# mLSTM encoder layer: new places for the mLSTM branch's blocks and the merged branches, and a longer, yielding filler

## The chip, the cores and the metric

The kernel runs on one core of one Trainium2 chip. The core's engines work side by side, each through its own queue in order: TensorE (PE, matmuls; PEld is its weight load), VectorE (DVE), ScalarE (ACT), GpSimd (POOL) and SyncE (SP), which here only issues DMAs. The metric is the device time of one execution in microseconds (us); lower is better.

## The reference, cut to what matters

One encoder layer over 1024 + 256 tokens (a prompt and a sample) of width 1024. An input projection feeds two branches; branch A is a gated convolution, branch B a chunkwise mLSTM that runs forward and backward, with 4 heads of 256 and chunks of 128 tokens (8 + 2 chunks). Each branch is projected, gated and added, and one output projection with a residual follows.

```python
h = rms_norm(x, norm_g) * (1.0 + scale) + shift
p = h @ w_in
cb, cc, cx, cz, q, k, v, o, mz, gpre, gmerge = split_combined(p)
y_conv = cb * centred_dwconv3(cc * cx, conv_w, conv_b) * silu(cz)
hm = h_fwd + h_bwd    # two mlstm_chunkwise scans over chunks of 128
hm = hm * rsqrt(mean(hm * hm) + EPS) * mh_norm_g
y_m = sigmoid(o) * hm * silu(mz)
merged = g_conv * (y_conv @ w_proj_conv) + g_mlstm * (y_m @ w_proj_mlstm)
return x + gate * (merged @ w_out)      # then a last rms_norm
```

In a scan each chunk reads the state C left by the chunk before it (`q @ C`) and then updates it, `C = decay * C + k^T (w v)`; inside a chunk, scores `q k^T` with a decay matrix weigh the values.

## The kernel before, in words

All data is float32; a product of two float32 matrices is made of three passes with the operands split into a high and a low part (`...H` and `...L`, `wh` and `wl`). ACT makes a high part by a cast, POOL or DVE the low part by a subtraction.

There are three stages. First, the input projection (about 1230 us), which leaves its results in DRAM: `qT_dr`, `kT_dr`, `v_dr`, `kn_dr` for the heads, `og_dr` for the gates of branch B, `yc_dr` for branch A's block, `th_dr` for the merge gates.

Second, the sweeps. Steps s = 0 to 54 are written out in the loop from line 1562. Each head has a first sweep of 10 chunks in one direction (steps 10h to 10h + 9), whose queries are kept in `kept`, and a second sweep in the other direction (steps 10h + 10 to 10h + 19). A step of a sweep has a query (`qc`, line 1277), a state product (`u`, line 1295) and the update of C on DVE (line 1303). The second sweep adds for each chunk the scores (line 1338), weighing, and, two steps later, the values (from line 1366); for each pair of chunks, four steps after its first, `finish` (from line 1399) normalises, transposes, multiplies with the gate (line 1428) and stores the pair's block to `ym_dr` (line 1435). So head 3 is in its second sweep in steps 40 to 49, and steps 50 to 54 only finish. It goes from chunk 9 down to chunk 0.

Heads 0 and 2 share one set of tiles, heads 1 and 3 another: `qTs`, `kTs`, `vNs` (loaded by `load_head`) and `kept`. They are made in the pool `qkv` from line 1220 on, which ends with the sweeps.

Between the sweeps' matmuls stands the filler (class `Filler`): branch A's projection, 32 units of 24 matmuls (line 1517). Unit u is token half b, output block n of 8, and quarter q: u = 16b + 2n + q. Its matmuls come in four parts of six (line 1526). The y blocks of branch A that it reads lie in tiles b00 and b10 (H and L); each pair of units has a gate tile `th` from a pool of three, which the unit's result multiplies (line 1530) and a DMA stores as `zc_dr` (line 1533). PACE (line 1551) says how many units may have been issued by step s.

`first_ym` (line 1535) prepares the second token half of branch B's y for the third stage: eight rows of 128 x 640 are loaded from `ym_dr` into buffers of the same `th` pool, cast to the high part by ACT (line 1543) and subtracted to the low part by DVE (line 1544). Rows 0 to 3 belong to heads 0 and 1, 4 and 5 to head 2, 6 and 7 to head 3. The results go to b00 and b10, after the filler's last read of them.

The order of all this on the engines is made by a planner, `Board` (line 41). It takes the operations with their durations (in the source), what each reads and writes, and the step at which each was written down. It goes through a modelled time, and each time finds the operation that can begin first; among those of the same engine that can begin within 0.25 us of it (SOON), it takes the one with the least (low, step, time). `low` marks operations that yield to all others. Buffers of a tag are given out in the order in which they were written down. The engines then run this order; only the weight and gate loads of the third stage are put between by the framework.

Third, the merge. `merge` (line 1639) multiplies y of branch B by `w_proj_mlstm` (`proj_y`, lines 1453 to 1455), adds branch A's `zc_dr`, and leaves the sum as `mH`, `mL` (line 1649); `finish` (line 1652) multiplies that by `w_out` and normalises. This is done for the second token half and then for the first, for which `load_y` loads y into b00 and b10.

Of the kernel before, what the change touches and what calls it, by code (L numbers as in the profile page):

```python
# [12 lines left out]
ALU = mybir.AluOpType  # L13
# [160 lines left out]
def encoder_kernel(  # L174
# [1040 lines left out]
    thp = ctx.enter_context(tc.tile_pool(name="thp", bufs=3, side="right"))  # L1215
    mstack = ctx.enter_context(ExitStack())
# [14 lines left out]
    board = Board()  # L1231
    op, buf = board.op, board.buf
# [9 lines left out]
    def piece(c):  # L1242
        return 0 if c < 5 else 1 if c < 8 else 2

    def load_head(h, n, which="qkv"):

        i, (c0, c1) = h % 2, PIECES[n]
        hs, ts_ = slice(h * HD, (h + 1) * HD), slice(c0 * P, c1 * P)
        kb = 128 * (c1 - c0)
        if "v" in which:  # L1250
            load(kb, lambda: vNs[i][:, c0:c1, 0:HD], v_dr[ts_, hs].rearrange("(c p) d -> p c d", p=P), (), [("vN", i, n)], h > 0)
        for nm, t, src in (("qT", qTs[i], qT_dr), ("kT", kTs[i], kT_dr)):
            if nm[0] in which:
                load(kb, lambda t=t: t[:, :, ts_], src[hs, ts_].rearrange("(b p) t -> p b t", p=P), (), [(nm, i, n)], h > 0)

    class Sweep:
# [12 lines left out]
        def query(self, c, dst, tok):  # L1269
            if c not in self.has_query:  # L1270
                return
            i, C = self.i, self.C
            pq = buf(psM, [P, 512], F32, "qc", 1)

            def mm():
                for kd in range(2):
                    PE.matmul(pq[:, 0:HD + 2], qTs[i][:, kd, c * P:(c + 1) * P], C[:, kd, :], start=kd == 0, stop=kd == 1)  # L1277

            op("PE", .88, mm, r=[("qT", i, piece(c)), C], w=[pq])
            op("ACT", .47, lambda: A.activation(dst(), pq[:, 0:HD + 2], AF.Copy, bias=0.0,  # L1280
                                                scale=gcol[:, 1, self.d, self.h, c:c + 1]), r=[pq], w=[tok])

        def state(self, c):
            if c not in self.has_state:
# [5 lines left out]
                                                scale=gcol[:, 3, self.d, h, c:c + 1]), r=[("vN", i, n)], w=[wv])  # L1290
# [16 lines left out]
    class Pairs:  # L1307
# [22 lines left out]
        def scores(self, c):  # L1330
# [9 lines left out]
            op("PE", .45, mm, r=[("qT", i, piece(c)), ("kT", i, piece(c))], w=[pS])  # L1340
# [8 lines left out]
            for d in (1 - self.d, self.d):  # L1349
                tok = [] if self.alone(d, c) else [(qcf, j) if d == self.d else ("kept", i, c)]  # L1350
                op("DVE", .43, lambda d=d: weigh(d), r=[pS, (abc, j)] + tok, w=[(den, j, d), (abc, j)])
# [14 lines left out]
        def values(self, c):  # L1366
# [12 lines left out]
               r=[Ps, ("vN", i, piece(c))], w=[pv])  # L1379
# [13 lines left out]
            if not self.alone(dk, c):  # L1393
                op("DVE", .5, two_, r=[r, ("kept", i, c)] + ([(qcf, j)] if fresh else [pv]), w=[(qcf, j)])
# [42 lines left out]

    def y_tile(n, part):
        return hp.tile([P, 4, TH2], F32R, tag=("b00", "b10")[n] + "HL"[part], name="y")
# [18 lines left out]
    class Filler:  # L1458
# [38 lines left out]
        def unit(self, after):  # L1497
# [37 lines left out]
    def first_ym(n):  # L1535

        y = [buf(hp, [P, 4, TH2], F32R, ("b00", "b10")[n] + part, 1) for part in "HL"]
# [13 lines left out]
    PACE = [min(4 + s, 12) if s < 10 else 12 + (s - 9) * 4 // 7 if s < 17 else 16 if s < 21 else min(17 + (s - 21) * 15 // 23, 32)  # L1551
# [10 lines left out]
    for s in range(10 * NH + 15):  # L1562
# [9 lines left out]
        if h < NH:  # L1572
            c, d = one[h].order[i], one[h].d
            one[h].query(c, lambda h=h, c=c, d=d: kept[h % 2][:, slot(d, c), :], ("kept", h % 2, c))
            one[h].state(c)
# [63 lines left out]
    def merge(t0, y, mH, mL):  # L1639
        for n, q, acc in proj_y(wpm, y, acc_d):  # L1640
# [8 lines left out]
            A.copy(mH[:, n, qs], th[:, qs])  # L1649
            V.tensor_tensor(out=mL[:, n, qs], in0=th[:, qs], in1=fp(mH[:, n, qs]), op=ALU.subtract)  # L1650

    def finish(c0, last, mH, mL):
# [8 lines left out]
        def product_o(pd, half, ws, j):  # L1661
            ts_ = slice(j * P, (j + 1) * P)
            for k in range(4):
                kt = 4 * half + k
                sH, sL = mH[:, kt, ts_], mL[:, kt, ts_]
# [111 lines left out]
```

## Time and profile before

| what | us |
|---|---|
| median of three runs | 1780.63 (1777.02 to 1780.88) |
| the profiled execution, whole | 1778.43 |
| its span, from the first to the last instruction | 1776.7 |
| sweeps: first state product to first matmul of the merge | 1239.65 to 1536.53 |
| first filler matmul | 1230.43 |
| last filler matmuls before the merge (start) | 1498.23 |

A row of the profile names the line, the engine, the operation, and out<-in by the program's names; in the timeline the two numbers in front are start and duration in us, x4 is a count of merged instructions, and brackets give the idle time of the engine before the row and who ended it. The slices of the page are each a fortieth of the span, 44.4 us. PEclk is the clock that PE was granted.

### The profile page before, as it was taken

What the parts mean: (1) busy time and instruction counts of PE and PEld (TensorE: products, weight loads), DVE (VectorE), ACT (ScalarE), POOL (GpSimd) and SP (SyncE); (2) the same over time, 40 slices, a digit from 0 to 9 for tenths busy, and PEclk for the clock granted to TensorE, in tenths of its full rate; (3) what the DMA queues carried; (4) which work ended last, traced back from release to release, by engine and by line L of the source; (5) the groups of instructions that cost most, each with busy time, mean ns of one, the idle gap of its engine ahead of it and who ended that gap; (6) DMA issues with size and microseconds to landing.
All of it is one profiled execution on the core that took longest, in us unless ns stands there. A gap on an engine that the chain in (4) does not pass through costs nothing.

```text
span 1776.7 us, 29030 instructions
## 1 busy us (share of the span) xinstructions
PE 1687.2 (95%) x11182; PEld 1623.0 (91%) x11182; DVE 953.7 (54%) x1703; ACT 620.7 (35%) x1243; POOL 697.4 (39%) x533
## 2 busy tenths in 40 slices
PE   4879999999988999999999999999999999799997
PEld 1679999999887999999999999999988998599997
DVE  6874333267888455554555423322257667556545
ACT  6552332223344322222222232222256555334223
POOL 2453333334444466666666533333210111123322
PEclk9889999999999999999999999999999999899999
DMA  7223332313555222212222234338779855563721
GB/s 304 76 70 122 107 100 95 105 60 104 149 162 141 87 77 66 71 59 63 77 67 74 99 103 129 96 103 282 259 238 297 262 179 181 175 215 116 254 97 72
DMA packets 213693, 239.58 MB, mean 135 GB/s; under 512 B 12356, under 2 KB 172340, under 8 KB 212532
## 3 DMA queue, kind: packets, MB, share of 16 engines
q1 hardware_dynamic: 213556, 237.74, 42.0%
q8 instruction: 88, 1.44, 0.3%
q14 instruction: 49, 0.40, 0.1%
HBM read 169.46 MB, written 68.23 MB: 134 GB/s over the span
## 4 chain that ended last, share of the span: by engine, by line
PE 63%; DVE 3%; issue 1%; ACT 1%; DMA 1%; POOL 0%; SPq 0%; ACTq 0%; DVEq 0%; POOLq 0%
PE accx L471 35%; PE qc L1277 3%; PE u L1295 3%; PE accd L1453 2%; PE accd L1454 2%; PE accd L1455 2%; PE accd L1667 2%; PE accd L1668 2%; PE accd L1666 2%; PE acc L1522 2%; PE acc L1523 2%; PE acc L1524 2%; PE misc L1378 1%; PE misc L1338 1%; DVE gacc L966 1%
## 5 line engine op out<-in xcount | busy, mean ns | idle before, releaser
L543 DVE TENSOR_TENSOR q<-accx,q 128x640 f32<-128x640 f32 x288 | 233.5, 821 | 477.4 <-PE accx L471 404.8
L293 POOL TENSOR_TENSOR wl<-comb,wh 128x512 fp32r<-128x512 f32 x176 | 237.0, 1349 | 486.5 <-ACT wh L292 441.7
L293 POOL TENSOR_TENSOR wl<-raw,wh 128x512 fp32r<-128x512 f32 x168 | 234.6, 1401 | 202.6 <-ACT wh L292 194.4
L471 PE MATMUL accx<-half,wh 128*128 128x320 f32 x1408 | 267.0, 312 | 7.0 <-ACT wh L292 5.4
L292 ACT CAST wh<-comb 128x512 fp32r<-128x512 f32 x176 | 108.7, 620 | 371.7 <-DVE comb L513 282.7
L471 PEld LDWEIGHTS accx<-half,wh 128*128 128x128 f32 x1408 | 222.4, 189 | 8.6 <-ACT wh L292 5.7
L471 PE MATMUL accx<-half,wl 128*128 128x320 f32 x704 | 161.6, 311 | 0.8 <-POOL wl L293 0.8
L292 ACT CAST wh<-raw 128x512 fp32r<-128x512 f32 (+1 forms) x184 | 119.4, 654 | 72.5 <-PE accd L1668 20.3
L632 ACT ACTIVATE q<-q,zero 128x640 f32<-128x640 f32 x80 | 66.4, 830 | 172.4 <-DVE q L543 155.7
L471 PEld LDWEIGHTS accx<-half,wl 128*128 128x128 f32 x704 | 118.5, 189 | 1.5 <-POOL wl L293 1.5
L1483 POOL TENSOR_TENSOR wl<-raw,wh 128x512 fp32r<-128x512 f32 x28 | 35.7, 1280 | 203.7 <-ACT wh L1482 182.2
L1667 PE MATMUL accd<-wl,mH 128*128 128x256 f32 x320 | 91.1, 285 | 0.1
L1668 PE MATMUL accd<-wh,mL 128*128 128x256 f32 x320 | 90.9, 284 | 0.0
L1666 PE MATMUL accd<-wh,mH 128*128 128x256 f32 x320 | 90.9, 285 | 0.0
L471 PE MATMUL accx<-b10H,wh 128*128 128x320 f32 x352 | 82.5, 316 | 6.7 <-ACT q L1070 5.9
L471 PE MATMUL accx<-t2H,wl 128*128 128x320 f32 x352 | 80.8, 311 | 5.4 <-POOL wl L293 5.4
L471 PE MATMUL accx<-b00H,wh 128*128 128x320 f32 x352 | 82.0, 314 | 2.3 <-DVE half L380 2.3
L471 PE MATMUL accx<-t2H,wh 128*128 128x320 f32 x352 | 81.1, 312 | 2.0 <-ACT wh L292 2.0
L471 PE MATMUL accx<-b10H,wl 128*128 128x320 f32 x352 | 81.2, 312 | 1.0 <-POOL wl L293 1.0
L471 PE MATMUL accx<-b00H,wl 128*128 128x320 f32 x352 | 81.0, 311 | 1.1 <-POOL wl L293 1.1
L471 PE MATMUL accx<-t3H,wl 128*128 128x320 f32 x352 | 80.5, 310 | 1.2 <-POOL wl L293 1.1
L471 PE MATMUL accx<-t3H,wh 128*128 128x320 f32 x352 | 80.5, 310 | 1.0 <-ACT wh L292 1.0
(315 smaller groups left out, 4227.8 us busy)
## 6 DMA issues: line engine op xcount, KB each, us to landing
raw<-in_w_in_dram SPq DMA_DIRECT2D x96, 256.0 KB
raw<-in_w_in_dram SPq DMA_DIRECT2D x44, 512.0 KB
th_dr<-q SPq DMA_DIRECT2D x32, 320.0 KB
th<-th_dr SPq DMA_DIRECT2D x32, 320.0 KB
wa<-in_w_ada_dram SPq DMA_DIRECT2D x8, 1024.0 KB
raw<-in_w_proj_conv_dram SPq DMA_DIRECT2D x16, 512.0 KB
k<-kn_dr SPq DMA_DIRECT2D x64, 128.0 KB
raw<-in_w_proj_mlstm_dram SPq DMA_DIRECT2D x16, 512.0 KB
```

What stands on the lines that cost most here:

```text
L292: A.copy(wh[:], src)
L293: eng.tensor_tensor(out=wl[:], in0=src, in1=fp(wh[:]), op=ALU.subtract)
L471: PE.matmul(acc[:, q, 0:TQ], st_[:, k, :], m_[:, q * TQ:(q + 1) * TQ], start=k == 0 and n == 0, stop=k == 3 and n == 2)
L543: V.tensor_tensor(out=two(dst), in0=ps, in1=two(t), op=ALU.add)
L632: A.activation(out, in_, AF.Tanh, bias=zero[:, 0:1], scale=0.5)
L1277: PE.matmul(pq[:, 0:HD + 2], qTs[i][:, kd, c * P:(c + 1) * P], C[:, kd, :], start=kd == 0, stop=kd == 1)
L1295: PE.matmul(pu[:, db, 0:HD + 2], k[:, db * P:(db + 1) * P], wv[:], start=True, stop=True)
L1453: PE.matmul(accs[q][:, :TQ], wh, yH, start=kt == 0, stop=False)
L1483: op("POOL", 1.36, lambda wh=wh, wl=wl, src=src: G.tensor_tensor(out=wl[:], in0=src(), in1=fp(wh[:]), op=ALU.subtract), r=[raw, wh], w=[wl])
L1666: PE.matmul(pd, sH, ws[0][:, k, :], start=kt == 0, stop=False)
L1667: PE.matmul(pd, sH, ws[1][:, k, :], start=False, stop=False)
L1668: PE.matmul(pd, sL, ws[0][:, k, :], start=False, stop=kt == KT - 1)
```

## The change

- The even heads' tiles (qT, kT, vN, kept) are made in a new pool `yq` that lasts to the kernel's end, under the tags y0 to y3; the odd heads' tiles stay in `qkv`. The planner now knows all eight as buffers.
- `first_ym` puts branch B's y into y0 to y3, once head 2 has been read for the last time, and `load_y` does so for the first token half.
- `mH` and `mL` are no longer tiles of their own in `mgp`: the merge writes them to b00 and b10.
- Units 22 to 31 of the filler are `low` on PE.
- PACE from step 21 on: 15 units over 29 steps instead of 23, so the last is issued at step 50, not 44.

```diff
+    board = Board()
+    op, buf = board.op, board.buf
+
+    yq = ctx.enter_context(tc.tile_pool(name="yq", bufs=1))
     mstack = ctx.enter_context(ExitStack())
     qkv = mstack.enter_context(tc.tile_pool(name="qkv", bufs=1))
...
-    kept = [qkv.tile([P, NC - 2, HD + 2], F32, name=f"kept{i}") for i in range(2)]
+    def resident(shape, nm, n):
+        res = []
+        for pool, tag in ((yq, f"y{n}"), (qkv, f"o{n}")):
+            res.append(buf(pool, shape, F32, tag, 1, pool.tile(shape, F32, tag=tag, name=nm)))
+        return res
+
+    qTs, kTs = resident([P, 2, T], "qT", 0), resident([P, 2, T], "kT", 1)
+    vNs, kept = resident([P, NC, HD + 2], "vN", 2), resident([P, NC - 2, HD + 2], "kept", 3)
...
-    kTs, vNs, qTs = [None, None], [None, None], [None, None]
-    for i in (1, 0):
-        kTs[i] = qkv.tile([P, 2, T], F32, name=f"kT{i}")
-        vNs[i] = qkv.tile([P, NC, HD + 2], F32, name=f"vN{i}")
-        qTs[i] = qkv.tile([P, 2, T], F32, name=f"qT{i}")
...
-                op("PE", .88, lambda part=part: mm(part), r=ops + ([acc] if part else []), w=[acc],
+                op("PE", .88, lambda part=part: mm(part), r=ops + ([acc] if part else []), w=[acc], low=u >= 22,
                    after=after if part == 0 else ())
...
-        y = [buf(hp, [P, 4, TH2], F32R, ("b00", "b10")[n] + part, 1) for part in "HL"]
+        y = [buf(yq, [P, 4, TH2], F32R, f"y{2 * n + part}", 1) for part in range(2)]
...
-    PACE = [min(4 + s, 12) if s < 10 else 12 + (s - 9) * 4 // 7 if s < 17 else 16 if s < 21 else min(17 + (s - 21) * 15 // 23, 32)
+    PACE = [min(4 + s, 12) if s < 10 else 12 + (s - 9) * 4 // 7 if s < 17 else 16 if s < 21 else min(17 + (s - 21) * 15 // 29, 32)
...
-            yH, yL = y_tile(n, 0), y_tile(n, 1)
+            yH, yL = (yq.tile([P, 4, TH2], F32R, tag=f"y{2 * n + part}", name="y") for part in range(2))
...
-            A.copy(mH[:, n, qs], th[:, qs])
-            V.tensor_tensor(out=mL[:, n, qs], in0=th[:, qs], in1=fp(mH[:, n, qs]), op=ALU.subtract)
+            mh, ml = (m[n // 4][:, n % 4, qs] for m in (mH, mL))
+            A.copy(mh, th[:, qs])
+            V.tensor_tensor(out=ml, in0=th[:, qs], in1=fp(mh), op=ALU.subtract)
...
-        mH = mgp.tile([P, KT, TH2], F32R, tag="mH", name="mH")
-        mL = mgp.tile([P, KT, TH2], F32R, tag="mL", name="mL")
+        mH, mL = ([hp.tile([P, 4, TH2], F32R, tag=b + part, name="m" + part) for b in ("b00", "b10")] for part in "HL")
```

The remaining hunks only rename: the strings that stood for the heads' tiles in the planner's lists become the buffers themselves.

More of the change, by code (lines that the diff above doesn't have):

```diff
@@ L1250, in load_head @@
         if "v" in which:
[L1251 to L1254, printed above, removed]
+            load(kb, lambda: vNs[i][:, c0:c1, 0:HD], v_dr[ts_, hs].rearrange("(c p) d -> p c d", p=P), (), [(vNs[i], n)], h > 0)
+        for nm, t, src in (("q", qTs[i], qT_dr), ("k", kTs[i], kT_dr)):
+            if nm in which:
+                load(kb, lambda t=t: t[:, :, ts_], src[hs, ts_].rearrange("(b p) t -> p b t", p=P), (), [(t, n)], h > 0)
     class Sweep:
@@ L1349, in scores @@
             for d in (1 - self.d, self.d):
-                tok = [] if self.alone(d, c) else [(qcf, j) if d == self.d else ("kept", i, c)]
+                tok = [] if self.alone(d, c) else [(qcf, j) if d == self.d else (kept[i], c)]
                 op("DVE", .43, lambda d=d: weigh(d), r=[pS, (abc, j)] + tok, w=[(den, j, d), (abc, j)])
@@ L1378, in values @@
             op("PE", .5, lambda: PE.matmul(pv[:, :HD], Ps[:], vNs[i][:, c, :HD], start=True, stop=True),
[L1379 removed]
+               r=[Ps, (vNs[i], piece(c))], w=[pv])
             d, dk = self.d, 1 - self.d
@@ L1393, in values @@
             if not self.alone(dk, c):
-                op("DVE", .5, two_, r=[r, ("kept", i, c)] + ([(qcf, j)] if fresh else [pv]), w=[(qcf, j)])
+                op("DVE", .5, two_, r=[r, (kept[i], c)] + ([(qcf, j)] if fresh else [pv]), w=[(qcf, j)])
             junk = buf(mp_, [P, HD], F32, "junk", 1)
@@ L1436, in finish @@
                    r=[(og, db)], w=[("ym", h, g, db)])
-    def y_tile(n, part):
-        return hp.tile([P, 4, TH2], F32R, tag=("b00", "b10")[n] + "HL"[part], name="y")
     def proj_y(src, y, acc_of):
@@ L1573, in encoder_kernel @@
             c, d = one[h].order[i], one[h].d
-            one[h].query(c, lambda h=h, c=c, d=d: kept[h % 2][:, slot(d, c), :], ("kept", h % 2, c))
+            one[h].query(c, lambda h=h, c=c, d=d: kept[h % 2][:, slot(d, c), :], (kept[h % 2], c))
             one[h].state(c)
@@ L1664, in product_o @@
                 kt = 4 * half + k
-                sH, sL = mH[:, kt, ts_], mL[:, kt, ts_]
+                sH, sL = mH[half][:, k, ts_], mL[half][:, k, ts_]
                 PE.matmul(pd, sH, ws[0][:, k, :], start=kt == 0, stop=False)
```

8 lines of the change are left out of this document (3 added, 5 removed).

## The prediction

> **What bounds the kernel now.** I read the page first: its busy shares, its slices, its chain.
>
> ```profile
> span 1776.7 us, 29030 instructions
> ...
> PE 1687.2 (95%) x11182; PEld 1623.0 (91%) x11182; DVE 953.7 (54%) x1703; ACT 620.7 (35%) x1243; POOL 697.4 (39%) x533
> ...
> PE   4879999999988999999999999999999999799997
> ...
> PEclk9889999999999999999999999999999999899999
> ...
> PE 63%; DVE 3%; issue 1%; ACT 1%; DMA 1%; POOL 0%; SPq 0%; ACTq 0%; DVEq 0%; POOLq 0%
> ```
>
> TensorE bounds nearly everything. Apart from the start and the very end, one slice (44 us each) is at 7 tenths, the 35th, and there the clock falls too. That is where the mLSTM sweeps run out and the merge begins, and where the change works. So next I asked for the busy time by stage (columns: window, length, then busy us and instructions of PE, PEld, DVE, ACT, POOL, then clock, DMA share, GB/s), and for the filler's accumulators alone.
>
> ```profile
> 1428.20:1469.60 41.40, 41.40 (x244) 38.12 (x243) 26.59 (x90) 23.41 (x60) 5.51 (x6) 1.00 0.53 164
> 1469.60:1498.80 29.20, 28.83 (x183) 27.08 (x182) 18.59 (x77) 16.69 (x46) 3.94 (x3) 1.00 0.51 162
> 1498.80:1518.00 19.20, 12.43 (x63) 9.62 (x61) 17.07 (x47) 10.36 (x27) 3.08 (x2) 1.00 0.56 183
> 1518.00:1536.50 18.50, 9.36 (x32) 5.01 (x32) 13.45 (x49) 9.22 (x26) 0.00 (x0) 0.78 0.45 134
> 1536.50:1542.10 5.60, 5.57 (x21) 5.58 (x22) 0.00 (x0) 0.00 (x0) 0.00 (x0) 0.52 0.81 240
> ```
> ```profile
> 1428.20:1469.60 41.40, 16.57 (x98) 14.40 (x96) 2.44 (x5) 1.00 0.53 164
> 1469.60:1498.80 29.20, 16.36 (x96) 14.40 (x96) 1.69 (x4) 1.00 0.51 162
> ```
>
> Up to 1498.8 PE is full because filler matmuls (98 and 96 in the two windows) stand between the mLSTM's. Then the filler is used up. In the last two sweep windows PE idles 6.8 + 9.1 = 15.9 us, with 0.4 us more just before. The timeline of PE shows with what it is idle:
>
> ```profile
> 1498.38 0.60 PE L1425 MATMUL misc<-ident,qcf 128*128 128x128 f32 x4
> 1498.82 1.04 PE L1277 MATMUL qc<-C,qT 128*128 128x258 f32 x4
> ...
> 1503.98 1.14 PE L1277 MATMUL qc<-C,qT 128*128 128x258 f32 x4 [1.20 <-DVE C L1303]
> ...
> 1506.92 1.11 PE L1277 MATMUL qc<-C,qT 128*128 128x258 f32 x4 [0.94 <-DVE C L1303]
> ...
> 1512.69 1.14 PE L1277 MATMUL qc<-C,qT 128*128 128x258 f32 x4 [2.62 <-DVE C L1303]
> ...
> 1518.02 1.14 PE L1277 MATMUL qc<-C,qT 128*128 128x258 f32 x4 [1.31 <-DVE C L1303]
> ...
> 1534.65 1.30 PE L1425 MATMUL misc<-ident,qcf 128*128 128x128 f32 x4 [3.33 <-ACT qcf L1418]
> 1536.53 0.64 PE L1453 MATMUL accd<-b00H,wh 128*128 128x320 f32 x1 [0.58 <-DVE og L1428]
> 1536.96 0.47 PE L1454 MATMUL accd<-b00L,wh 128*128 128x320 f32 x1
> ...
> 1541.49 0.47 PE L1453 MATMUL accd<-b10H,wh 128*128 128x320 f32 x1
> ```
>
> Head 3's last queries are 3 to 6 us apart (steps 45 to 49), each after the C update. From 1518 a pure chain runs through PE, DVE and ACT to the last gated block, and the merge's first matmul waits for that. The merge then starts at half clock: 17 matmuls from 1536.96 to 1541.49 are 0.267 us apart.
>
> **The change, part by part.** Price of a filler unit, from an uninterrupted one:
>
> ```profile
> 1234.03 0.31 PE L1522 MATMUL acc<-y,wh 128*128 128x320 f32 x1
> ...
> 1237.40 0.31 PE L1524 MATMUL acc<-y,wl 128*128 128x320 f32 x1
> 1239.65 1.11 PE L1295 MATMUL u<-wv,k 128*128 128x258 f32 x4 [1.94 <-DMA th<-th_dr]
> ```
>
> 24 matmuls, 23 spacings in 3.37 us: 0.147 each, 3.52 us a unit.
>
> *Pace.* PACE reaches 32 units at step 44 before (23 x 15 // 23 = 15) and at step 50 after (29 x 15 // 29). By PACE, units 28 to 31 (14.1 us of PE) are released at steps 45, 47, 49 and 50 instead of 41 to 44. Units from 22 on are also low: the planner takes them only where no sweep operation can start within 0.25 us. Ten units, 35 us, become stuffing for whatever gap there is from step 33 on, and the sweeps run ahead of them. No instruction is added; PE's work is the same, so what can be won is idle time and lost clock:
> - idle from 1469.6 to 1536.5: 0.4 + 6.8 + 9.1 = 16.3 us;
> - the merge's first 20 matmuls at full clock: 20 x (0.267 - 0.147) = 2.4 us;
> - the sweeps' last matmuls at clock 0.78: 9.36 x 0.22 = 2.1 us.
>
> Together 20.8 us, the ceiling: 1778.4 - 20.8 = 1757.6.
>
> *Can the sweep chain end earlier?* It must, as the merge waits for it. In 1428.2 to 1469.6 (steps 33 to 38 and the start of 39) 98 filler matmuls take 14.4 us; without them the sweeps need 27 us of PE. From there to step 45 they need 29.2 - 14.1 = 15.1 us, 3 us a step. After 1498.8 DVE is the busy one, 17.1 of 19.2 us, and here the y conversion is in the way:
>
> ```profile
> 1499.77 3.49 DVE L1544 TENSOR_TENSOR b00L<-th,b00H 128x640 fp32r<-128x640 f32 x2
> 1503.18 0.74 DVE L1303 SCALAR_TENSOR_TENSOR C<-C,decay,u 128x516 f32<-128x516 f32 x1
> ...
> 1507.50 1.56 DVE L1544 TENSOR_TENSOR b00L<-th,b00H 128x640 fp32r<-128x640 f32 x2
> ...
> 1512.81 0.82 DVE L1544 TENSOR_TENSOR b10L<-th,b10H 128x640 fp32r<-128x640 f32 x1
> ...
> 1531.75 0.82 DVE L1544 TENSOR_TENSOR b10L<-th,b10H 128x640 fp32r<-128x640 f32 x1
> ```
> ```profile
> 1499.50 3.08 POOL L293 TENSOR_TENSOR wl<-raw,wh 128x512 fp32r<-128x512 f32 x2 [14.48 <-ACT wh L292]
> ```
>
> So the chain has slack to give: 27 us up to step 39, 3.5 to 4 us for each of 40 to 49 (between the 2.94 us from 1503.98 to 1506.92 and the 5.3 us from 1512.69 to 1518.02) and some 17 for the rest (18.5 now, at low clock) end it at 1507 to 1512, left alone. Each of its PE steps can stand behind one filler part of 6 matmuls (0.88 us) that it cannot interrupt; over 15 steps that is up to 13 us. I take 1521 to 1530 for the merge's start, 1525 as the middle: 11.5 us gained.
>
> *Places of y.* The mLSTM half of y went into b00/b10, which the filler read until its last unit; hence the subtractions only from 1499.8 on. Now it goes where head 2's qT, kT, vN and kept were, free after step 41. Without this the later filler would push y behind it. Costs: the same 8 loads, 8 ACT casts, 8 DVE subtractions; but they share the three th buffers with the filler.
>
> ```profile
> 1474.33 0.33 SPq L1235 DMA_DIRECT2D th<-ym_dr  x1
> ...
> 1501.48 2.60 SPq L1235 DMA_DIRECT2D th<-ym_dr  x3
> ...
> 1524.73 0.80 SPq L1235 DMA_DIRECT2D th<-ym_dr  x2
> ```
>
> A pass through the buffers, from issue to the end of the subtraction, takes 7.6 to 7.8 us (1501.48 to 1507.50 + 1.56; 1524.73 to 1531.75 + 0.82). Before, all three buffers were free for it after the last unit. After, the th tiles of blocks 14 and 15 (units 28 to 31) stand in the row among the eight loads, and are held until units 29 and 31 are stored. Bounds: nothing, if the six loads that need no block of head 3 are through by then; two passes, 15 us, if one buffer carries the last of them. I take 1 us, nearer the first end, since six loads can spread over 30 us, and keep the other for the range.
>
> *SP.* The raws and th loads move in the queue with their units; they were never what PE waited for after 1300 (its releasers in the tail are DVE and ACT). The last filler store (zc) comes later, but the merge reads it seven blocks of two units on, 49 us later: nothing.
>
> *Merged blocks to b00/b10.* Same instructions; they wait for the filler's last read, which stands earlier on PE than the merge's first result: nothing. In the second half they wait for the first half's output product, as the old tiles did.
>
> *Layout at the stage's start.* Head 0's tiles move to the front of the freed space, which the t1/t4 blocks held longest.
>
> ```profile
> 1217.90 12.78 SPq L589 DMA_DIRECT2D qT_dr<-q  x4
> 1230.78 0.38 SPq L1235 DMA_DIRECT2D vN<-v_dr  x1
> ```
> ```profile
> 1225.79 0.45 PE L471 MATMUL accx<-b11H,wh 128*128 128x320 f32 x2
> ```
>
> The last product reads b11 alone, from 1225.79, so those blocks are free then; head 0's first load stands behind the queue's stores until 1230.78 anyway: nothing. If it slipped, the first u at 1239.65, where PE already idles 1.9 us, would slip with it, at most by the 3.5 us that one product lasts.
>
> Sum: -11.5 (start of the merge) - 2.4 (clock) + 1 (y) = -12.9, from the profiled execution's 1778.4 (span 1776.7 and 1.7 around it): 1765.5. The median shown, 1780.6, is 2.2 above that execution; half of it put on gives **1767**, rounded.
>
> **The rivals.**
> 1. *Only part is won.* The chain, slowed behind filler parts and DVE, ends at 1530 to 1535: gain 1.5 to 6.5, with 2.4 of clock and the same 1.1 put on, 1771 to 1776. For it: DVE was 89% busy in steps 45 to 49. Against: 5.9 us of that were y subtractions, which can now lie elsewhere.
> 2. *Slower: y is late.* Mechanism: the th row. If the sweeps starve the low units so long that buffers come free only with the last units (about 1518), eight loads need three passes of 7.7 us, 23 us: y is whole at 1541, PE stands idle till then, and the merge, of whose first unit the last half reads the later blocks, loses 3 to 5 us against 1536.5 and begins at half clock; with one to four of the subtractions stretched beside POOL as the pair at 1499.77 was, 0.9 us each, 1784 to 1788. It decides from where the first y load is issued after about 1513 (1536.5 - 23; before, at 1474).
> 3. *No change.* The chain's latency, not the work, sets 1536: the planner's order, kept by every engine, holds a sweep operation behind filler as long as it gained. 1777 to 1784. Against it: steps at 2.94 us where DVE is free.
>
> On rivals 1 and 2: the two subtractions beside POOL's split at 1499.50 took 3.49 us as a pair, 0.9 us each over the 0.82 of the others. The later filler brings its last splits into the tail; four subtractions stretched so are 3.7 us on DVE, 1770 instead of 1767 if all of it lies on the chain. The Trainium skill, GPSIMD Engine Reference, section Specifications, says that GpSimd shares its SBUF interfaces with VectorE and contends with DVE instructions that read two SBUF inputs, as these do; the trace agrees, with that pair, and by the rule every overlap of the later splits with a subtraction would cost again.
>
> **How the numbers follow.** Forecast (start at 1521 to 1530: 1762 to 1771) 0.50; rival 1 0.20; no change 0.15; slower 0.15. A measurement of this kernel tells about 0.2% (3.6 us) from no change. Faster 0.50 + 0.20 = 0.70, same 0.15, slower 0.15. The range runs from the ceiling, 1758, to 1780, half of the no-change case; above it lie about 0.2.
>
> **What would show it.** Right: filler matmuls (L1522 to L1524 now) among PE's rows up to within 5 us of the merge; PE idle under 5 us in the last 40 us of the sweeps; clock near 1.0 there; the first merge matmul near 1525 with 0.147 us spacing. Step "chain ends earlier" is wrong if the last gated block (L1428) still ends near 1536; "y costs 1" is wrong if the first merge unit waits for y's casts or subtractions. Wrong altogether: idle PE before 1300 grows (layout), or waits appear after 1542.

## The result, and the profile after

The changed kernel takes 1767.67 us, the median of four runs (1767.08 to 1768.56); the kernel before, run beside it, 1780.64 (1777.02 to 1780.88). The ratio is 0.9932, 95% interval [0.9919, 0.9944]: 0.7% less time. The profiled execution took 1767.08 us; the one before took 1778.43, so 11.35 us are to be found in the two traces.

The page of the changed kernel: span, busy time of the engines, slices of PE and its clock.

```profile
span 1765.1 us, 29030 instructions
...
PE 1681.6 (95%) x11182; PEld 1620.9 (92%) x11182; DVE 958.9 (54%) x1703; ACT 620.4 (35%) x1243; POOL 696.7 (39%) x533
...
PE   4879999999988999999999999999999999899997
...
PEclk9889999999999999999999999999999999899999
```

The 35th slice rose from 7 to 8 tenths, but the clock dips there as before. PE in windows of 20 us (busy, instructions, clock, DMA share, GB/s), of the kernel before and then after:

```profile
1420.00:1440.00 20.00, 20.00 (x120) 1.00 0.82 260
...
1480.00:1500.00 20.00, 19.64 (x126) 1.00 0.41 121
1500.00:1520.00 20.00, 12.48 (x62) 1.00 0.58 187
1520.00:1540.00 20.00, 11.59 (x40) 0.70 0.50 154
```
```profile
1420.00:1440.00 20.00, 18.96 (x101) 1.00 0.66 199
1480.00:1500.00 20.00, 20.00 (x130) 1.00 0.42 128
1500.00:1520.00 20.00, 17.77 (x116) 1.00 0.64 195
1520.00:1540.00 20.00, 14.13 (x77) 0.74 0.90 291
```

PE's idle time in 1500 to 1520 fell from 7.5 to 2.2 us. In 1420 to 1440, where PE was full, 1.0 us of idle time has appeared. From 1520 on PE still idles, at a low clock. The timeline of PE after shows one hole in place of the many small waits:

```profile
1517.99 0.31 PE L1523 MATMUL acc<-b10H,wh 128*128 128x320 f32 x1
...
1525.30 1.30 PE L1429 MATMUL misc<-ident,qcf 128*128 128x128 f32 x4 [6.71 <-ACT qcf L1422]
1527.17 0.64 PE L1454 MATMUL accd<-y,wh 128*128 128x320 f32 x1 [0.58 <-DVE og L1432]
...
1531.34 0.47 PE L1454 MATMUL accd<-y,wh 128*128 128x320 f32 x1
...
1532.45 0.31 PE L1454 MATMUL accd<-y,wh 128*128 128x320 f32 x1
```

The filler now lasts until 1518.6, 20 us longer. Then PE waits 6.71 us for the scaling of the last pair (`qcf`, line 1422 now), and the merge starts at 1527.17, 9.4 us earlier than the 1536.53 of before. Its matmuls are again at half clock (0.47 us long, 0.267 apart) until about 1531.9. What held the scaling stands in ACT's and DVE's timelines and in the chain of waits:

```profile
1519.64 0.60 ACT L292 CAST wh<-raw 128x512 fp32r<-128x512 f32 x1
1524.11 0.72 ACT L1544 CAST y<-th 128x640 fp32r<-128x640 f32 x1 [3.86 <-DMA th<-ym_dr]
1524.74 0.91 ACT L1422 ACTIVATE qcf<-qcf,rstm 128x256 f32<-128x256 f32 x2
```
```profile
1522.03 0.16 DVE L1417 TENSOR_TENSOR rstm<-rs_t,rs_r 128x2 f32<-128x2 f32 x1
```
```profile
1516.18 0.62 ACT wh L292
...
1516.87 1.87 POOL wl L293
...
1518.76 0.38 SPq L282
...
1519.25 4.83 DMA th<-ym_dr
...
1524.11 0.72 ACT y L1544
1524.83 0.42 ACT qcf L1422
...
1525.30 0.89 PE misc L1429 x2
```

The scaling needs `rstm`, which DVE had ready at 1522.19. It ran at 1524.74, because ahead of it in ACT's queue stood a cast of one of branch B's y rows, and that cast waited for its row. Read backwards, the row was issued at 1519.25, behind a weight load of the merge (line 282) on SP's queue, which had waited for its buffer until POOL's split ended at 1518.74. So 2.5 us of the hole are not the chain's own: an operation that nobody needed yet stood at the head of an in-order queue.

The rest of the gain lies where no wait is. The output product's groups, before and after (busy, mean ns of one, idle before):

```profile
L1667 PE MATMUL accd<-wl,mH 128*128 128x256 f32 x320 | 91.1, 285 | 0.1
```
```profile
L1669 PE MATMUL accd<-wl,mH 128*128 128x256 f32 x320 | 89.6, 280 | 0.1
```

Matmul to matmul, these were 120.0 ns apart and are now 117.3. Where each phase starts (first matmul, us):

| phase | before | after |
|---|---|---|
| merge, second token half | 1536.53 | 1527.17 |
| output product | 1595.34 | 1585.88 |
| merge, first token half | 1652.93 | 1642.20 |
| output product | 1709.24 | 1698.71 |
| last matmul | 1766.99 | 1755.53 |

The first output product takes 57.59 before and 56.32 after, the second 57.75 and 56.82: 2.2 us together. The first merge takes as long as before (58.81 and 58.71). So of the 11.35 us, 9.4 are won at the merge's start, 2.2 in the output products, and 0.2 are lost between.

### The profile page after: what moved, and what is told of

The parts are those of the page before. It is cut to its first block, busy times and chain, and to the rows that moved or that the text cites. A ratio compares the mean times of both kernels' runs of the same rounds, so it can differ in the third digit from the quotient of the medians.

```text
span 1765.1 us, 29030 instructions
## 1 busy us (share of the span) xinstructions
PE 1681.6 (95%) x11182; PEld 1620.9 (92%) x11182; DVE 958.9 (54%) x1703; ACT 620.4 (35%) x1243; POOL 696.7 (39%) x533
## 4 chain that ended last, share of the span: by engine, by line
PE 63%; DVE 3%; DMA 1%; issue 1%; ACT 1%; POOL 0%; SPq 0%; DVEq 0%; ACTq 0%; POOLq 0%
PE accx L471 36%; PE qc L1281 3%; PE u L1299 3%; PE accd L1454 2%; PE accd L1455 2%; PE accd L1456 2%; PE accd L1669 2%; PE accd L1670 2%; PE accd L1668 2%; PE acc L1523 2%; PE acc L1524 2%; PE acc L1525 2%; PE misc L1382 1%; PE misc L1342 1%; DVE gacc L966 1%
## 5 line engine op out<-in xcount | busy, mean ns | idle before, releaser
L471 PE MATMUL accx<-b11H,wl 128*128 128x320 f32 x352 | 80.3, 309 | 1.1 <-POOL wl L293 1.1
```

The costliest lines, as they stand in the source:

```text
L471: PE.matmul(acc[:, q, 0:TQ], st_[:, k, :], m_[:, q * TQ:(q + 1) * TQ], start=k == 0 and n == 0, stop=k == 3 and n == 2)
```

## The experiments

The change has three parts that can be set apart: the **places** (y in the even heads' tiles, `mH` and `mL` in b00 and b10), the **pace** (15 units over 29 steps instead of 23) and the **yielding** (`low` for units 22 and up). After the first four runs the questions were the late y row, the hole before the merge, and the faster output product. Each kernel was timed against the kernel before on the same chip; its median there lay between 1778.9 and 1780.6 us. Diffs are against the changed kernel unless said.

| kernel | median us | ratio to before, 95% interval | merge starts | longest hole before it | PE idle, 1240 to merge | first merge lasts |
|---|---|---|---|---|---|---|
| before | 1780.6 | | 1536.53 | 3.3 | 20.6 | 58.8 |
| after | 1767.67 | 0.9932 [0.9919, 0.9944] | 1527.17 | 6.7 | 14.9 | 58.7 |
| places alone | 1774.07 | 0.9966 [0.9953, 0.9978] | 1533.24 | 3.3 | 16.3 | 58.1 |
| pace and yielding | 1768.69 | 0.9928 [0.9909, 0.9947] | 1527.11 | 5.4 | 14.5 | 59.0 |
| places and pace | 1771.86 | 0.9951 [0.9935, 0.9966] | 1530.94 | 4.1 | 17.1 | 58.3 |
| places and yielding | 1761.64 | 0.9895 [0.9879, 0.9911] | 1522.06 | 3.7 | 10.2 | 58.0 |
| yielding alone | 1766.20 | 0.9928 [0.9913, 0.9942] | 1523.06 | 5.1 | 12.7 | 58.9 |
| after, y rows in buffers of their own | 1764.95 | 0.9920 [0.9905, 0.9935] | 1524.14 | 4.4 | 12.0 | 58.3 |
| faster pace, more units yield | 1757.33 | 0.9872 [0.9855, 0.9888] | 1515.74 | none | 5.0 | 60.4 |
| the same, y rows in own buffers | 1757.77 | 0.9883 [0.9866, 0.9899] | 1519.31 | none | 7.8 | 56.6 |

The idle time is the windows' length less PE's busy time, from 1240 to the merge's first matmul: before 296.53 - 275.89, after 287.17 - 272.30.

### One part or two at a time

Places alone:

```diff
-  ..., w=[acc], low=u >= 22,
+  ..., w=[acc],
-  ... else min(17 + (s - 21) * 15 // 29, 32)
+  ... else min(17 + (s - 21) * 15 // 23, 32)
```

> The changed kernel with the old pace (15 units over 23 steps) and no yielding units: only the places are new. Theory (places and pace need each other): the filler is again used up about 38 us before the merge, PE idles 12 to 16 us in that tail, the y subtractions leave the C chain, so the merge starts 1 to 4 us before 1536.5: 1773 to 1778 us. Rival 'the places alone make the gain, by taking y out of the tail': 1767 to 1770. If the output product (57.6 us before, 56.3 after, in the first half) is short here too, 2 us of the gain belong to the places.

Measured: 1774.07 us, 5.0 less than the 1779.04 of before beside it. This is what its theory expected. The filler's last matmul starts about where it did (1499.47 and 1498.23), the merge begins 3.3 us earlier, and the first output product runs at 117.3 ns, as after. So the places bring time by themselves, in two ways. The product is faster. And y's subtractions begin at 1480.4 instead of 1499.8, so fewer of them lie among the last C updates on DVE; from 1440 on, PE's queries (`qc`) wait 1.3 us for the C update, once, where in the kernel before they wait 6.1 us in four pieces.

Pace and yielding, with the places of before (diff against the kernel before):

```diff
-  ..., w=[acc],
+  ..., w=[acc], low=u >= 22,
-  ... else min(17 + (s - 21) * 15 // 23, 32)
+  ... else min(17 + (s - 21) * 15 // 29, 32)
```

> The kernel before with the new pace and the yielding units, y still in b00 and b10. Theory: y can be written only after the filler's last unit, which now comes at about 1518, so eight casts and subtractions stand between it and the merge: merge at 1532 to 1545, 1776 to 1788 us. Rival 'the filler's order alone makes the gain': merge at 1527, 1767 to 1771. Output product 57.6 us as before if its length comes from the places.

Measured: 1768.69 us, as the rival expected and not the theory; the merge begins at 1527.11, when the changed kernel's does. Here y goes to b00 and b10 only after the late filler's last read, and its last subtraction is far behind the merge's start, in DVE's timeline and PE's:

```profile
1535.24 1.38 DVE L1544 TENSOR_TENSOR b10L<-th,b10H 128x640 fp32r<-128x640 f32 x1 [2.04 <-ACT b10H L1543]
```
```profile
1527.11 0.63 PE L1453 MATMUL accd<-b00H,wh 128*128 128x320 f32 x1 [1.13 <-DVE og L1428]
...
1531.28 0.47 PE L1453 MATMUL accd<-b10H,wh 128*128 128x320 f32 x1
1531.55 0.47 PE L1453 MATMUL accd<-b00H,wh 128*128 128x320 f32 x1
```

The merge doesn't stop for it: after the blocks that are there it goes on with b00 for the second pair of accumulators (1531.55), and comes to the last rows of b10 when they are done. Here y was whole 9.5 us after the merge's start, and no matmul of the merge waited for it.

Places and pace, without the yielding:

```diff
-  ..., w=[acc], low=u >= 22,
+  ..., w=[acc],
```

> The changed kernel with no yielding units: new places, new pace. Theory: units 28 to 31 still lie in the tail and fill it, but stand ahead of the sweeps; the chain ends later than with yielding units, merge at 1528 to 1533, 1768 to 1774 us. Rival 'yielding does all': as with the places alone, 1773 to 1778.

Measured: 1771.86 us, within its theory's 1768 to 1774. Against places alone it is 2.2 us less, but the two intervals overlap. PE's idle time up to the merge is no smaller (17.1 against 16.3 us). Nothing more than a small gain can be put down to the pace.

Places and yielding, with the old pace:

```diff
-  ... else min(17 + (s - 21) * 15 // 29, 32)
+  ... else min(17 + (s - 21) * 15 // 23, 32)
```

> The changed kernel with the old pace and yielding units from 22 on. Theory: a unit released early but yielding lands in the same gaps, so within 3 us of the changed kernel: 1765 to 1771 us. Rival 'the pace decides': the filler is used up earlier and 5 us or more of idle PE come back, 1772 to 1778.

Measured: 1761.64 us, ratio 0.9895 [0.9879, 0.9911], below the changed kernel's interval and faster than theory and rival expected. The slower pace is thus a loss of some 6 us inside the change. In the windows of this kernel 1420 to 1440 is full again, and the idle time from 1440 on is 5.84 us (9.01 in the changed kernel):

```profile
1240.00:1440.00 200.00, 195.65 (x1122) 177.67 (x1121) 112.46 (x368) 101.16 (x258) 25.55 (x20) 1.00 0.80 259
1440.00:1522.06 82.06, 76.22 (x470) 70.22 (x468) 64.42 (x216) 45.40 (x125) 13.82 (x10) 1.00 0.51 158
1420.00:1440.00 20.00, 20.00 (x109) 17.75 (x108) 16.06 (x59) 14.61 (x40) 0.00 (x0) 1.00 0.72 217
```

The 6 us have several parts. By the two profiled executions, PE idles with the old pace 1.5 us less up to 1440 and 3.2 us less from there to the merge, of which 3.05 are a shorter hole (3.66 against 6.71), and the first merge is 0.7 us shorter. So an early offer fills early gaps, but that is the smaller part here: half of the loss is the longer hole, of which 2.5 us are the late row's. The other pairs of yielding kernels that differ by the pace alone point the same way, but weakly. With the old places (1768.69 and 1766.20) and with y rows in buffers of their own (1764.95 and 1763.34, both below) the old pace is ahead by 2.5 and 1.6 us only, with intervals that overlap.

Yielding alone (diff against the kernel before):

```diff
-  ..., w=[acc],
+  ..., w=[acc], low=u >= 22,
```

> The kernel before with yielding units from 22 on and nothing else: old pace, old places. Theory now (the yielding alone wins, the new pace costs, the places give 2 us in the output product and little else): merge at 1521 to 1525, output product 57.6 us, 1762 to 1767 us. Rival (places are needed once the units yield): merge at 1527 or later, 1769 to 1776.

Measured: 1766.20 us, 13.7 less than the 1779.89 of before beside it. One word does what the whole change does (0.9928 against 0.9932), at the old places and the old pace. The hole before its merge is 5.14 us. Its first output product runs at 118.7 ns, between the two others, though `mH` and `mL` lie where they lay before; nothing here explains that.

### What the hole before the merge is

All kernels with a hole wait there for the last pair's scaling. Four runs looked for what can shorten it.

The y rows in three buffers of their own, so that the filler's `th` row doesn't hold them, first in the changed kernel:

```diff
-            raw = buf(thp, [P, TH2], F32, "th", 3)
+            raw = buf(thp, [P, TH2], F32, "yraw", 3)
```

> The changed kernel as it is (new pace, yielding), with three buffers of its own for the rows of y. In the changed kernel the last scaling on ACT stands behind a cast of y that waits 3.9 us for its row, and the row's load behind a weight load that waits for POOL. If that row makes the hole of 6.7 us before the last transposes, the rows come earlier here, the cast waits for nothing, and the merge starts 2 to 5 us earlier (1522 to 1525), 1762 to 1766 us. If it was only the last of several equal waits: within 1.5 us, 1766 to 1769.

Measured: 1764.95 us, 2.7 less than the changed kernel's median, within its first reading's 1762 to 1766, though the intervals overlap. The trace says what happened: no cast waits ahead of the last scaling, the hole is 4.35 us instead of 6.71, and the merge begins at 1524.14 instead of 1527.17:

```profile
1522.26 1.30 PE L1429 MATMUL misc<-ident,qcf 128*128 128x128 f32 x4 [4.35 <-ACT qcf L1422]
```

The same with the old pace:

```diff
-  ... else min(17 + (s - 21) * 15 // 29, 32)
+  ... else min(17 + (s - 21) * 15 // 23, 32)
-            raw = buf(thp, [P, TH2], F32, "th", 3)
+            raw = buf(thp, [P, TH2], F32, "yraw", 3)
```

> The changed kernel with the old pace, and three buffers of its own for the rows of y, out of the filler's gate ring. If the shared ring holds y, and by it the last casts and the chain's scaling behind them: y's last subtraction 5 us earlier or more, merge 2 to 4 us earlier, 1758 to 1760 us. If late y is covered, since the merge starts with the blocks that are there: within 1.5 us of the old pace alone, 1760 to 1763.

Measured: 1763.34 us, 0.9908 [0.9889, 0.9927]: no gain over places and yielding (1761.64). The hole is 4.35 us against 3.66, and the merge begins 1.6 us later. So the first reading didn't come. In places and yielding the last scaling waits 1.55 us on ACT for DVE's `rstm`, not behind a row: there was nothing to take away. The row in ACT's way belongs to the slow pace. Of those 1.55 us, 0.87 are one small DVE instruction (`rs_t`, 1.03 us for its usual 0.16) that ran beside a split on POOL; the last section comes back to this.

The merge's first accumulators in other banks of PSUM (the memory that matmuls write to) than the sweeps' last transposes, in the old pace:

```diff
-    psB = bstack.enter_context(tc.tile_pool(name="psB", bufs=3, space=PSUM))
     psM = bstack.enter_context(tc.tile_pool(name="psM", bufs=1, space=PSUM))
+    psB = bstack.enter_context(tc.tile_pool(name="psB", bufs=3, space=PSUM))
...
+  ... else min(17 + (s - 21) * 15 // 23, 32)
```

> The changed kernel with the old pace, and the PSUM banks given to the sweeps in another order, so that the merge's first accumulators get the banks of the queries, states and filler, and not those of the last transposes. If the merge waits for the last gated block only because it takes its bank, its first matmuls move into the hole of 5 us before it: merge at 1517 to 1519, full clock, 1755 to 1760 us. If it waits for data (y) or for its place in the order: same as with the old pace alone, 1761 to 1763.

Measured: 1762.24 us, the same as without (1761.64). The merge still waits 0.58 us for the last gated block (`og`), and the hole of 3.66 us is still there. In its profiled execution, the fastest of its four (1759.76), the merge begins 2.2 us earlier, at 1519.86, but lasts 0.8 us longer (58.86 against 58.02), since the granted clock is 0.50 for the first 5.0 us of it, and for 3.2 us there; nothing here says why it begins earlier. A shared bank as the reason of the wait is unlikely: with the banks in the old order, the first matmul of the faster pace below waits the same 0.58 us for the last reader of the filler's accumulators (`th`, line 635), so it seems to wait for whichever reader of the sweeps' PSUM comes last.

One unit held back until after step 50, to fill the hole, in the old pace:

```diff
-  ... else min(17 + (s - 21) * 15 // 29, 32)
+  ... else min(17 + (s - 21) * 15 // 23, 31 + (s > 50))
```

> The changed kernel with the old pace, but unit 31 alone held back to step 51, behind the last transpose of weights. If idle PE time is what is left to win, its four parts (3.5 us) fill the hole of 5.7 us between the last filler and the merge, the chain before it is 3.5 us less crowded, merge at 1519 to 1521 and near full clock: 1757 to 1760 us. If the chain's own latency sets its end: 1761 to 1763.

Measured: 1762.77 us, 0.9905 [0.9890, 0.9920]: the same. The filler ends 1.0 us later (1517.41 against 1516.39), the merge begins 1.0 us later, and the hole is 3.7 us as it was: the unit went in front of the hole, not into it.

### Why the output product is faster

The high half of the merged branches back in `mgp`, as two tiles of its own, the low half left in b00 and b10:

```diff
-  mH, mL = ([hp.tile([P, 4, TH2], F32R, ...) for b in ("b00", "b10")] for part in "HL")
+  mH, mL = ([(mgp if part == "H" else hp).tile([P, 4, TH2], F32R, ...) for b in ("b00", "b10")] for part in "HL")
```

> The changed kernel with the high half of the merged branches in new tiles beside the residuals, as before the change, and the low half in b00 and b10. If it is the place of the merged branches that shortens the output product: 57.0 to 57.6 us again instead of 56.3, 1768 to 1769 us. If it is the place of the output weights, or the number of tiles: 56.3, 1767.

Measured, in one execution: 1768.37 us against 1767.08 for the changed kernel's profiled execution. The product's matmuls are 120.0 ns apart again in the mean, and the first product takes 57.59 us, as before:

```profile
L1670 PE MATMUL accd<-wh,mL 128*128 128x256 f32 x320 | 91.4, 286 | 0.0
L1669 PE MATMUL accd<-wl,mH 128*128 128x256 f32 x320 | 90.9, 284 | 0.1
```

So the place of `mH` goes with the 2.2 us, and all ten kernels that have it in b00 and b10 take 56.32 us for the first product. But the place is not the whole cause. The yielding alone gave 118.7 ns at the old place. The spacings repeat 121, 119 ns in the kernel before and 118, 118, 124 here: the same mean by another pattern. And the spacing changes within a run, with `mH` where it lay: near the end of the second product PE loses about 0.4 us waiting for a low half of the weights, and the last 90 matmuls behind that are 118.7 ns apart both in the kernel before (120.0 up to there) and in the changed one (117.3), but still 117.4 in the faster pace below. What sets the pattern stays open.

### A better version

If early offers are better than late ones, the pace should go the other way, with more units yielding:

```diff
-  ..., w=[acc], low=u >= 22,
+  ..., w=[acc], low=u >= 18,
-  ... else min(17 + (s - 21) * 15 // 29, 32)
+  ... else min(17 + (s - 21) * 15 // 18, 32)
```

> The changed kernel with a faster pace than the old one (15 units over 18 steps) and units yielding from 18 on. Theory (a yielding unit should be offered early, since the planner can only fill a gap with what has been released): as good as the old pace or better, 1759 to 1763 us. Rival (the filler is used up before the tail, where the gaps are): an idle tail of 4 us or more comes back, 1765 to 1772.

Measured: 1757.33 us, 0.9872 [0.9855, 0.9888], 10.3 us below the changed kernel and better than the theory's 1759 to 1763. The pace and the number of yielding units change together here, so the share of each isn't known. The last filler matmul starts at 1514.85 and the merge begins at 1515.74, with no hole and at full clock. The windows of this kernel (columns as in the prediction), and the row of PE's waits from 1500 to 1560 that matters (us in total, times, longest):

```profile
1240.00:1440.00 200.00, 195.81 (x1118) 176.52 (x1117) 116.14 (x380) 101.82 (x263) 22.93 (x18) 1.00 0.79 257
1440.00:1515.74 75.74, 74.98 (x467) 69.71 (x466) 55.21 (x200) 41.11 (x113) 13.83 (x11) 1.00 0.50 155
1515.74:1576.11 60.37, 57.66 (x385) 56.59 (x385) 33.80 (x55) 22.11 (x37) 19.09 (x14) 1.00 0.84 287
```
```profile
PE accd L1454 <- ACT y L1544: 2.5, 2, 1.4
```

From 1440 to the merge only 0.76 us of PE are idle. Now the merge does wait for y, 2.5 us in two pieces. That this wait can be taken away was the last run's question: the same kernel with the y rows in buffers of their own.

```diff
-            raw = buf(thp, [P, TH2], F32, "th", 3)
+            raw = buf(thp, [P, TH2], F32, "yraw", 3)
```

> d_fast (units released over 18 of the steps, units 18 and up yielding) with three buffers of their own for branch B's y rows, as in e_rawbuf. In d_fast the merge begins at 1515.7, before y is whole: its matmuls wait 2.5 us in two pieces for the casts, and the casts wait for rows that come through the filler's buffers. If the row through the shared buffers is what makes y late there, the casts and subtractions come earlier, no matmul of the merge waits for the casts (0 to 0.3 us in place of 2.5), the merge lasts 58 us in place of 60.4, and the time is 2 to 3 us under d_fast's 1757.3: 1754 to 1755.5. If y is late because head 3's blocks themselves are late (its chain then ends just before the merge), the casts wait as long as before, the merge stays at 60 us and the time at 1757 to 1758.

Measured: 1757.77 us, 0.9883 [0.9866, 0.9899]: no faster. The wait is gone, as the first reading expected, and the merge takes 56.62 us, all of it busy; but it begins 3.6 us later:

```profile
1240.00:1440.00 200.00, 194.53 (x1100) 174.87 (x1099) 114.49 (x378) 101.80 (x263) 22.95 (x18) 0.99 0.80 259
1440.00:1519.31 79.31, 76.97 (x485) 71.49 (x483) 62.33 (x208) 46.40 (x124) 14.83 (x11) 1.00 0.53 167
1519.31:1575.93 56.62, 56.62 (x385) 56.62 (x385) 28.09 (x48) 17.34 (x30) 18.94 (x13) 1.00 0.83 274
```

Its idle time from 1240 to the end of that merge is 335.93 - 328.12 = 7.8 us; without the buffers it is 336.11 - 328.45 = 7.7. With other buffers the planner makes another order of the sweeps, which leaves the gaps in them instead (5.5 us up to 1440 where there were 4.2, 2.3 after it where there were 0.8). What was won at y was lost there. The two are the best kernels of the series and can't be told apart.

## Why the prediction was right, and where it was not

The forecast was 1767 us; the median is 1767.67. The sum, 1765.5, stands against the profiled 1767.08. Single terms are further off, and partly cancel:

| term of the sum | predicted | measured |
|---|---|---|
| start of the merge | -11.5 | -9.4 |
| clock at the merge's start | -2.4 | -0.1 |
| y through the `th` row | +1 | inside the start: 2.5 us of the hole |
| output product | 0 | -2.2 |
| other phases | 0 | +0.3 |
| sum | -12.9 | -11.4 |

- **What bounds the kernel** was right. Most of the gain came from the sweeps' tail, from idle PE, and the ceiling of 20.8 us was a fair one: the faster pace with more yielding units reached 1757.46 in its profiled execution, against the 1757.6 of the ceiling (with 2.2 us from the products, which the ceiling did not hold).
- ***Pace*: half right, and the wrong half was the edit itself.** "Ten units, 35 us, become stuffing for whatever gap there is from step 33 on, and the sweeps run ahead of them": that is what yielding does, alone 13.7 us. But the prediction took the later release as part of the gain. Measured, it costs some 6 us with the new places (1761.64 with the old pace), half of it by the longer hole in which the late row stands. A smaller slip: by PACE, units 28 to 31 were released at steps 40, 41, 43 and 44 before, not 41 to 44.
- ***Chain ends earlier***: mechanism right, the start within the 1521 to 1530 given, 2.2 us later than its middle. The estimate that the chain left alone ends at 1507 to 1512 fits the faster pace, whose last gated transposes start at 1510.7. Of the rows named as proof, the filler among PE's rows "to within 5 us of the merge" (8.6 us) and "PE idle under 5 us" (8.1 us in the last 40) didn't come.
- ***Clock*: this term failed.** The prediction counted 2.4 us for a merge that starts at full clock, and this needed a sweep's end without a hole. One of 6.71 us was left, and the first merge took 58.71 us in place of 58.81. That the size was about right is seen where no hole is left: 56.62 us with the faster pace and own buffers, 2.1 less.
- ***Places of y***: "Without this the later filler would push y behind it" is wrong as a reason. y is late with the old places, but the merge begins at the same 1527.1, since it takes the blocks that are there first. What the places bring by themselves was left out: 3.3 us at the merge's start and the product's speed. Added to the yielding they bring 4.6 us at the old pace (1766.20 to 1761.64, with intervals apart), but about 1 us at the slow one (1768.69 to 1767.67, not to be told from nothing): there the late row takes back what they win.
- ***y costs 1 us***: the right suspicion (the `th` row), the wrong victim. No unit of the merge waited for y. But a row that came late held ACT's queue, and behind it stood the last scaling: 2.5 us. The prediction asked who waits for y, not who stands behind it.
- ***SP: nothing***: not quite. The chain of waits leads through a weight load on SP's queue to that late row.
- ***Merged blocks: nothing*** was right for waits (the phases follow each other without a gap), wrong for time: 2.2 us, from the same matmuls at another place. That such matmuls can run at two speeds was in the trace before (120.0 ns, and 118.7 for the last 90), but not which of them a new place would give.
- ***Layout at the start: nothing*** held: PE's idle time from 1240 to 1300 is 2.31 us in both traces. Up to 1440 it grew by 1.5 us, but from the slower pace, for with the old pace it is 4.35 against the 4.33 of before.
- **Rival 1** (part won, 1771 to 1776) is what places and pace give without the yielding: 1771.86. **Rival 2** (y late) didn't come; first y loads were issued at 1486.1. **Rival 3** (the planner's order gives back what it gained) holds in the small: the last run's order did that.
- **The splits beside the subtractions**, weighed at 3.7 us: none of the eight subtractions was stretched, but five other instructions of DVE between 1498 and 1522 were, by 0.4 to 1.0 us each and 4.4 us together (below). The size was near, the operations that it struck were other ones. How much of it the merge's start pays isn't known: the last scaling of the changed kernel waited for the row, not for DVE.

So the total was right, the main mechanism too, and its precision was luck: a start 2.1 us short and a clock term of 2.3 us that failed, against one of 2.2 us that nobody had counted and the 1 us set aside for y.

## What to carry to other kernels

Work that stuffs gaps should be made to yield, which alone brought 13.7 us here, and offered no later than the gaps come: in no pair of these kernels did the later release gain anything once the units yielded. An operation that nobody needs yet can still be the bound if it waits at the head of an in-order queue, so ask of each moved load who stands behind its consumer, not only who needs the result. Where one engine is nearly full, take the sum of its gaps over the whole stretch as the measure: a wait that is removed in one place (2.5 us here) came back in another.

## What the runs showed of the hardware

**DVE and POOL wait for each other by whole instructions.** Three of the five stretched rows of DVE in the changed kernel, two rows that were not, and POOL's splits beside them:

```profile
1500.22 1.11 DVE L1408 TENSOR_SCALAR ssqm<-ssqm 128x2 f32<-128x2 f32 x1
...
1510.89 1.38 DVE L1376 SCALAR_TENSOR_TENSOR Pt<-abc,r,Pt 128x128 f32<-128x128 f32 x1
...
1512.26 0.34 DVE L1376 SCALAR_TENSOR_TENSOR Pt<-abc,r,Pt 128x128 f32<-128x128 f32 x1
...
1517.75 0.48 DVE L1388 SCALAR_TENSOR_TENSOR qcf<-qcf,r,misc 128x256 f32<-128x256 f32 x1 [0.15 <-PE misc L1382]
...
1520.51 1.10 DVE L1414 TENSOR_TENSOR rs_t<-rs_r 128x2 f32<-128x2 f32 x1
```
```profile
1500.01 1.30 POOL L1484 TENSOR_TENSOR wl<-raw,wh 128x512 fp32r<-128x512 f32 x1 [0.26 <-ACT wh L1483]
...
1510.71 1.41 POOL L293 TENSOR_TENSOR wl<-raw,wh 128x512 fp32r<-128x512 f32 x1 [2.37 <-ACT wh L292]
1516.87 1.86 POOL L293 TENSOR_TENSOR wl<-raw,wh 128x512 fp32r<-128x512 f32 x1 [4.75 <-ACT wh L292]
1520.32 1.26 POOL L293 TENSOR_TENSOR wl<-raw,wh 128x512 fp32r<-128x512 f32 x1 [1.59 <-ACT wh L292]
```

`Pt` takes 1.38 us in place of 0.34 and ends 0.15 us after the split beside it (1512.27 and 1512.12); the tiny `rs_t` (0.16 us in the kernel with own buffers) takes 1.10 and ends 0.03 after its split (1521.61 and 1521.58). The stretch is what is left of POOL's instruction, whatever DVE's own size. The other two of the five, `Pt` at 1498.52 and `r` at 1507.78, end 0.15 and 0.02 us after their splits. The scaled addition at 1517.75, whose second tensor (`misc`) comes from PSUM, keeps its 0.48 us in the midst of the split of 1516.87. The Trainium skill, SBUF — State Buffer, section "Who interferes with whom", says that the port pair shared by DVE and GpSimd is an exclusive lock and that a DVE instruction with two SBUF inputs contends with a GpSimd instruction that reads SBUF; these rows agree. Two tensor inputs are not the whole condition, though: `ssqm` at 1500.22 has one tensor and took 1.11 us in place of 0.16, ending 0.02 us after its split. The other direction shows in four splits that began while a subtraction ran. With 0.73, 0.36, 0.26 and 0.08 us of it left they took 1.86, 1.51, 1.41 and 1.26 us; the longest, at 1516.87 beside the subtraction from 1516.78 to 1517.60, stands in the chain before the merge.

**When the clock halves.** The granted clock of the changed kernel was 0.50 from 1521.59 to 1531.83. It fell 3.0 us into the hole of 6.71 us and came back 6.5 us after PE's first instruction behind it. In all these traces the times at which it changes lie whole multiples of 3.41 us apart, here three; of the last stretch of 3.41 us before the fall PE was busy 12%, and the last before the return was the first behind the hole in which it was busy throughout (the one before it, 74%). The Trainium skill, TensorE: Matmul & The Clock Gate, section "What's actually happening", puts both the idle window that closes the gate and the busy one that opens it at about 3.4 us; the changed kernel agrees with both lengths. But a hole of that length isn't needed. In places and pace, without the yielding, the clock fell at 1517.57, and no idle time in the 3.41 us before was longer than 1.36 us:

```profile
1517.40 0.35 PE L1379 MATMUL misc<-ident,Pt 128*128 128x128 f32 x1 [1.36 <-DVE Pt L1376]
1517.49 0.54 PE L1523 MATMUL acc<-b00H,wh 128*128 128x320 f32 x1
1517.83 0.47 PE L1524 MATMUL acc<-b00L,wh 128*128 128x320 f32 x1
```

PE was busy 47% of that stretch, with small matmuls and transposes. In the faster pace two waits of 1.14 and 1.40 us within the merge left the clock at 1.00, with PE busy about 60% or more of every such stretch. Where the line lies the runs can't tell: 58% was halved once (y rows in own buffers, at 1384.39) and 49% was not (places and yielding, from 1515.03 to 1518.44).

**The same matmul at several speeds.** 128x256 matmuls were 120.0, 118.7 or 117.3 ns apart in the mean, at full clock and without a wait between, steady over hundreds of them. Putting `mH` back in its old pool brought 117.3 back to 120.0; behind a wait near the end of the second product, both 120.0 and 117.3 became 118.7. The cause is open.
